# All tokens in grid order, and two groups' values projected with x as the stationary operand

## The chip, the cores and the metric

The kernel runs on one core of one Trainium2 chip. The metric is the device time of one execution in microseconds (us), the median of several runs. The profile is of one further execution, taken by the hardware profiler.

## The reference

Two layers of a bidirectional encoder over 1024 tokens of width 1024, in float32. The tokens form a grid of 16 rows of 64. Each layer projects the normed x into four head groups, attends in each, mixes the four outputs and runs a squared-ReLU MLP.

```python
for l in range(DEPTH):                       # 2
    h = rms_norm(x, norm1_g[l])
    proj = h @ w_in[l]                       # 1024 x 2400
    a_cq, a_ckv, a_kr, b_q, b_k, b_v, c_q, c_k, c_v, d_q, d_k, d_v = split(proj)
    y_a = mla_mixer(...)     # A: 4 heads, latent queries and keys, all 1024 keys
    y_b = diff_mixer(...)    # B: 4 heads, two softmaxes each, all 1024 keys
    y_c = swa_mixer(...)     # C: 4 heads, keys within 128 tokens of the query
    y_d = na_mixer(...)      # D: 4 heads, 8 rows x 16 columns of the 64-wide grid
    mix = concat([rms_norm(y_a), y_b, rms_norm(y_c), rms_norm(y_d)])
    x = x + mix @ w_out[l]
    x = x + square(relu(rms_norm(x, norm2_g[l]) @ w_up[l])) @ w_down[l]
return rms_norm(x, final_norm_g)
```

A, B and D don't care in which order the tokens stand, if the rotary tables, the masks and the result follow it. C is banded in natural order. D becomes banded with blocks of 128 when the tokens are put in grid order: eight columns of the grid (16 rows each) to a block.

## The kernel before

**Precision.** Every wide operand is kept as two float32r parts, high and low (`wh`, `wl` for weights, `xh`, `xl` for x, `both` for results on their way to DRAM). `passes` issues three matmuls for one product: high by high, high by low, low by high. ScalarE makes the high part (a copy), VectorE or GpSimd the low part (a subtraction).

**Projection.** x lies transposed in SBUF as eight pairs of tiles `xh`/`xl` of 128 features by 1024 tokens. `one(t, xs, ev)` projects 128 columns of `w_in`: two loads of 256 KB into `ws` (two buffers), split into `wh`/`wl`, and for each half of the tokens 24 matmuls with the weights stationary and 512 tokens moving, into one PSUM bank (`bank`, eight in all). The result is transposed, features by tokens. An eviction function takes it from there: `ev_rope` multiplies it with the rotary tables (`tabc`, `tabs`, which hold 1/rms of the tokens too) and adds; `ev_plain` multiplies with 1/rms (`rb`); `ev_grid` does the same for D and puts the tokens in grid order on the way. Queries and keys then go to DRAM (`qb`, `kb`, `qd`, ...) by `to_parts`. Values are needed with tokens on the partitions, so `to_values` transposes each half with four TensorE transposes against `ident` (`bank<-ident,part` in the profile), copies them out of PSUM on ScalarE and stores them (`vb`, `vd`, `vc`, `va`).

**Stages of a layer.** `open` computes the first wave: three weight tiles at once into six banks (`WAVES[0]`: B's queries, keys and values of heads 0 and 1), in two halves of the features, while the squares of x are summed; 1/rms (`rstd_cols`, `spread_here`) is known only when that is well under way, and the tables can be multiplied only then. `b1` is the second wave, `lat`, `pd`, `pc` the projections of A, D and C, `up` A's second stage; `b`, `d`, `c`, `a` are the attentions, `o1`, `o2` the output projection, then the MLP.

**Order.** All instructions are first recorded, with a due time for each stage (`SPAN`). A planner (`Plan.order`) then lists them engine by engine, by its own cost model and the due times, with a limited number of SBUF slots and PSUM banks. What it lists is fixed: on the chip each engine runs its list in order, and an instruction that waits holds all behind it. Every instruction is issued through one helper, so that all of them carry line 677 in the profile.

## Time and profile before

| | |
|---|---|
| time, median of 3 runs | 2522.41 us (2521.24 to 2526.48) |
| the profiled execution's own time | 2517.78 us |
| its span | 2516.0 us |
| TensorE (PE) busy | 2467.4 us, 98% |
| VectorE (DVE) busy | 1909.8 us, 76% |
| ScalarE (ACT) busy | 1290.5 us, 51% |
| GpSimd (POOL) busy | 379.7 us, 15% |
| DMA | 378.56 MB, 150 GB/s |

In the rows of the profile, PE is a matmul and PEld the load of its stationary operand; `bank<-xh,wh` is a matmul that reads the tiles xh and wh and writes a PSUM bank. In a timeline the columns are start, duration, engine, line, operation, names, shapes and, in brackets, how long the engine stood idle just before and what ended that. The first layer's attention and output projection take about 0 to 600 us, the second layer's 1250 to 1840 us; the MLPs lie between and behind.

### The profile page before, as it was taken

What the parts mean: (1) busy time and instruction counts of PE and PEld (TensorE: products, weight loads), DVE (VectorE), ACT (ScalarE), POOL (GpSimd) and SP (SyncE); (2) the same over time, 40 slices, a digit from 0 to 9 for tenths busy, and PEclk for the clock granted to TensorE, in tenths of its full rate; (3) what the DMA queues carried; (4) which work ended last, traced back from release to release, by engine and by line L of the source; (5) the groups of instructions that cost most, each with busy time, mean ns of one, the idle gap of its engine ahead of it and who ended that gap; (6) DMA issues with size and microseconds to landing.
All of it is one profiled execution on the core that took longest, in us unless ns stands there. A gap on an engine that the chain in (4) does not pass through costs nothing.

```text
span 2516.0 us, 35396 instructions
## 1 busy us (share of the span) xinstructions
PE 2467.4 (98%) x12332; PEld 1967.1 (78%) x12332; DVE 1909.8 (76%) x3576; ACT 1290.5 (51%) x2397; POOL 379.7 (15%) x258
## 2 busy tenths in 40 slices
PE   8999999999999999999999999999999999999998
PEld 6777776778888887888877777677788888888887
DVE  7767867775877779888777677677678777898887
ACT  4545757653644445444425456666455444444454
POOL 3323224213000000000042231332140000000000
PEclk9999999999999999999999999999999999999999
DMA  5534478622244457444154344885123444665431
GB/s 180 180 112 133 122 218 234 197 80 72 78 165 159 151 202 271 147 142 139 72 182 130 119 117 135 232 255 170 46 70 117 155 155 158 231 231 158 130 105 67
DMA packets 190514, 378.56 MB, mean 150 GB/s; under 512 B 24112, under 2 KB 36352, under 8 KB 190336
## 3 DMA queue, kind: packets, MB, share of 16 engines
q1 hardware_dynamic: 175360, 350.09, 44.6%
q10 hardware_dynamic: 14976, 26.22, 2.7%
q8 instruction: 97, 1.59, 0.3%
q14 instruction: 81, 0.66, 0.1%
HBM read 260.15 MB, written 116.07 MB: 150 GB/s over the span
## 4 chain that ended last, share of the span: by engine, by line
PE 83%; DVE 8%; DMA 4%; ACT 2%; issue 2%; SPq 1%; POOL 0%; DVEq 0%; POOLq 0%; ACTq 0%
PE bank L677 83%; DVE p L677 2%; DVE part L677 1%; SPq L677 1%; ACT p L677 1%; DVE x L677 1%; DMA a<-in_w_down 1%; DVE sq L677 1%; DMA acts<-ev 1%; DVE col L677 0%; DMA latp<-lat 0%; DMA c<-in_w_down 0%; DVE xl L677 0%; DVE ev L677 0%; DVE both L677 0%
## 5 line engine op out<-in xcount | busy, mean ns | idle before, releaser
L677 PE MATMUL bank<-far,wh 128*128 128x512 f32 (+1 forms) x2848 | 870.3, 387 | 1.1 <-ACT wh L677 0.6
L677 PEld LDWEIGHTS bank<-far,wh 128*128 128x128 f32 x2848 | 532.4, 188 | 110.5 <-ACT wh L677 1.4
L677 PE MATMUL bank<-far,wl 128*128 128x512 f32 (+1 forms) x1424 | 550.3, 387 | 2.7 <-DVE wl L677 2.7
L677 ACT ACTIVATE p<-p,col 128x1024 f32<-128x1024 f32 (+2 forms) x320 | 294.6, 921 | 196.3 <-DVE col L677 194.2
L677 POOL TENSOR_TENSOR wl<-ws,wh 128x512 fp32r<-128x512 f32 (+1 forms) x138 | 191.1, 1390 | 1180.2 <-ACT wh L677 1089.8
L677 PEld LDWEIGHTS bank<-far,wl 128*128 128x128 f32 x1424 | 267.4, 188 | 57.9 <-DVE wl L677 3.4
L677 PE MATMUL bank<-stack 96*128 96x512 f32 (+2 forms) x896 | 285.0, 395 | 5.0 <-DVE col L677 2.3
L677 DVE TENSOR_TENSOR x<-bank,x 128x512 f32<-128x512 f32 (+1 forms) x276 | 187.2, 680 | 121.9 <-PE bank L677 121.0
L677 PE MATMUL bank<-ident,p 128*128 128x128 f32 x1376 | 253.6, 276 | 10.4 <-DVE part L677 4.8
L677 PE MATMUL bank<-xh,wh 128*128 128x512 f32 x608 | 250.9, 413 | 3.1 <-ACT wh L677 2.6
L677 PE MATMUL bank<-xh,wl 128*128 128x512 f32 x608 | 250.6, 413 | 1.1 <-POOL wl L677 1.1
L677 PE MATMUL bank<-xl,wh 128*128 128x512 f32 x608 | 250.6, 412 | 0.0
L677 PEld LDWEIGHTS bank<-ident,p 128*128 128x128 f32 x1376 | 171.3, 141 | 59.5 <-issue 10.7
L677 PEld LDWEIGHTS bank<-stack 96*128 96x128 f32 (+1 forms) x896 | 159.3, 189 | 43.8 <-DVE col L677 12.1
L677 ACT ACTIVATE pt<-bank 128x512 f32<-128x512 f32 (+2 forms) x256 | 137.5, 556 | 82.9 <-PE bank L677 75.2
L677 DVE TENSOR_TENSOR wl<-raw,wh 128x512 fp32r<-128x512 f32 x224 | 150.3, 690 | 34.5 <-ACT wh L677 34.0
L677 PE MATMUL bank<-pt,v 128*64 128x256 f32 (+2 forms) x1344 | 173.1, 396 | 2.2 <-ACT pt L677 2.0
L677 ACT ACTIVATE ev<-ev 128x512 f32<-128x512 f32 x128 | 80.6, 632 | 160.3 <-DVE ev L677 155.8
L677 DVE CUSTOM_DVE_ANT_0 p<-bank,zero,col 128x512 f32<-128x512 f32 x192 | 143.8, 749 | 22.2 <-PE bank L677 5.1
L677 PE MATMUL bank<-mix,wh 128*128 128x512 f32 x512 | 160.3, 393 | 0.0
L677 DVE CUSTOM_DVE_ANT_0 p<-bank,zero 128x512 f32<-128x512 f32 x192 | 131.7, 686 | 35.4 <-PE bank L677 34.1
L677 ACT ACTIVATE wh<-raw 128x512 fp32r<-128x512 f32 x224 | 135.4, 621 | 23.8 <-ACT ev L677 10.5
(158 smaller groups left out, 3904.5 us busy)
## 6 DMA issues: line engine op xcount, KB each, us to landing
act<-acts SPq DMA_DIRECT2D x224, 256.0 KB
raw<-in_w_up SPq DMA_DIRECT2D x128, 256.0 KB
acts<-ev SPq DMA_DIRECT2D x128, 256.0 KB
acts<-ev ACTq DMA_DIRECT2D x96, 256.0 KB
ws<-in_w_in SPq DMA_DIRECT2D x76, 256.0 KB
c<-in_w_down SPq DMA_DIRECT2D x64, 256.0 KB
rz<-drows SPq DMA_DIRECT2D x40, 256.0 KB
ws<-in_w_out SPq DMA_DIRECT2D x40, 256.0 KB
```

Source lines behind the costliest of these rows:

```text
L677: getattr(s.eng.engine, s.op)(*[real(a) for a in s.args], **{k: real(a) for k, a in s.kw.items()})
```

## The change

x is put in grid order on the host, and the result is put back there. The rotary tables follow the same order. So D needs no reordering at its evictions (`ev_grid` goes, `ev_plain` takes its place), while C is put back in natural order at its own evictions: `ev_rope` and the new `ev_rows` collect two halves and write with a strided pattern (`by_rows`). The strided copies of the attention output and of the denominators (`rows_of`) move from D to C.

B's and D's values are no longer projected as four weight tiles (`T_BV`, `T_DV`). `values` loads their 512 columns as eight tiles `wv` of 128 features, all held at once, and for each of eight blocks of 128 tokens issues 24 matmuls with x stationary and the 512 weight columns moving. The result has tokens on the partitions already, so that no transpose follows; ScalarE takes it out of PSUM and multiplies with 1/rms, which is now one number per partition. The first wave gets B's second query tile in place of the values; `b1` has `values` and B's second key tile. `vb` and `vd` are stored as blocks of 128 tokens by 256 columns, and a head's values are loaded from there in pieces of 64 numbers (`head_of`).

```diff
-T_BQ, T_BK, T_BV = (3, 6), (4, 7), (5, 8)
-T_DQ, T_DK, T_DV = (9, 12), (10, 13), (11, 14)
+T_BQ, T_BK = (3, 5), (4, 6)
+T_DQ, T_DK = (7, 9), (8, 10)
...
+def grid_order():
+    return np.arange(S).reshape(16, 8, 8).transpose(1, 0, 2).ravel()
...
-    t = np.arange(S, dtype=np.float32)
+    t = grid_order().astype(np.float32)
...
-    out["x"] = i["x"][0].T.reshape(8, P, S)
+    out["x"] = i["x"][0].T[:, grid_order()].reshape(8, P, S)
+    out["w_v"] = np.concatenate([i["w_in"][:, :, c:c + 256] for c in (864, 2144)], 2).reshape(n, 8, P, 512)
...
-        qb, kb, vb = dr([2, 2, 4, 16, 2, S], "qb"), dr([2, 2, 4, 16, 2, S], "kb"), dr([4, P, 8, 64], "vb")
+        qb, kb, vb = dr([2, 2, 4, 16, 2, S], "qb"), dr([2, 2, 4, 16, 2, S], "kb"), dr([8, P, 256], "vb")
...
-                yield from one(T_DQ[t], xs, self.ev_grid(rb, self.to_parts(qd[:, t], 0.125)))
-                yield from one(T_DK[t], xs, self.ev_grid(rb, self.to_parts(kd[:, t])))
-                yield from one(T_DV[t], xs, self.ev_grid(rb, self.to_values(vd[2 * t:2 * t + 2])))
+                yield from one(T_DQ[t], xs, self.ev_plain(rb, self.to_parts(qd[:, t], 0.125)))
+                yield from one(T_DK[t], xs, self.ev_plain(rb, self.to_parts(kd[:, t])))
+
+        def values(r):
+            ws = []
+            for k in range(8):
+                st = self.wp.tile([P, 512], F, tag="ws", bufs=2, name="ws")
+                self.load(st, d["w_v"][l, k])
+                w = self.place.tile([P, 2, 512], R, tag="wv", bufs=8, name="wv")
+                self.split(w[:, 0], w[:, 1], st, eng=nc.gpsimd)
+                ws.append((w[:, 0], w[:, 1]))
+            for t in range(8):
+                ps, at = self.mm_ps(), slice(t * P, t * P + P)
+                for k, (x, w) in enumerate(zip(xs, ws)):
+                    self.passes(ps, (x[0][:, at], x[1][:, at]), w, slice(0, 512), k == 0, k == 7)
+                v = self.part()
+                nc.scalar.activation(v, ps, AF.Copy, scale=r[:, t:t + 1])
+                for dst, c in ((vb, 0), (vd, 256)):
+                    self.keep(dst[t], v[:, c:c + 256])
...
-                yield from one(T_CQ2[t], xs, self.ev_rope(tabs, qc[:, t]))
-            yield from one(T_CK, xs, self.ev_rope(tabs, kc))
-            yield from one(T_CV, xs, self.ev_plain(rb, self.to_values(vc)))
+                yield from one(T_CQ2[t], xs, self.ev_rope(tabs, qc[:, t], True))
+            yield from one(T_CK, xs, self.ev_rope(tabs, kc, True))
+            yield from one(T_CV, xs, self.ev_rows(rb, self.to_values(vc)))
...
-            for ev, b in zip(evacs_b(0), banks):
+            for dst, b in zip((qb[:, 0], kb[:, 0], qb[:, 1]), banks):
+                ev = self.ev_rope(tabs, dst)
...
-            for t, ev in zip(self.WAVES[1], evacs_b(1)):
-                run_all(one(t, xs, ev))
+            values(r)
+            run_all(one(T_BK[1], xs, self.ev_rope(tabs, kb[:, 1])))
...
-    WAVES = [(T_BQ[t], T_BK[t], T_BV[t]) for t in range(2)]
+    WAVES = [(T_BQ[0], T_BK[0], T_BQ[1])]
...
-        return self.place.tile([P, 512], F, tag="part", bufs=3, name="part")
+        return self.place.tile([P, 512], F, tag="part", bufs=4, name="part")
...
+    def by_rows(self, ys, n, *halves):
+        for i, y in enumerate(ys):
+            o = y.rearrange("p (r b c) -> p b r c", r=8, b=8)[:, n * 4:n * 4 + 4]
+            yield (o, *(t.rearrange("p (b r c) -> p b r c", b=4, r=16)[:, :, 8 * i:8 * i + 8] for t in halves))
...
+            for o, a, b in self.by_rows(ys, n, t1, t2):
+                self.tt(o, a, b, ALU.add, self.eng)
...
+    def head_of(self, v, h):
+        return v[:, :, h * 64:h * 64 + 64].rearrange("t p d -> p t d")
...
-            v = self.vtile(vb[2 * t + h2])
+            v = self.vtile(self.head_of(vb, 2 * t + h2))
...
-    return np.ascontiguousarray(y.reshape(DM, S).T)[None]
+    out = np.empty((1, S, DM), np.float32)
+    out[0, grid_order()] = y.reshape(DM, S).T
+    return out
```

Three places show what the planner makes of it. The first is TensorE in the first layer, around the end of the first wave. Before, a second weight tile follows the wave (`bank_107<-xh_275,wl` is of its second half of tokens), and the four transposes of B's values stand in its midst:

```order
L677 MATMUL bank_107<-xl_288,wh 128x512
L677 MATMUL bank_107<-xh_275,wl 128x512
L677 MATMUL bank_101<-ident,part 128x128 x4
L677 MATMUL bank_107<-xh_292,wh 128x512
L677 MATMUL bank_107<-xl_308,wh 128x512
```

After, the wave's last matmul (`bank_106<-xh_352,wl`) is followed by the first matmuls of `values`, each into another bank; banks 101 to 106 are those of the wave:

```order
L683 MATMUL bank_106<-xh_352,wl 128x512
L683 MATMUL bank_100<-wv,xh_239 128x512
L683 MATMUL bank_107<-wv,xh_239 128x512
L683 MATMUL bank_101<-wv,xh_239 128x512
L683 MATMUL bank_102<-wv,xh_239 128x512
L683 MATMUL bank_103<-wv,xh_239 128x512
L683 MATMUL bank_100<-wv,xh_239 128x512
L683 MATMUL bank_100<-wv,xl_245 128x512
L683 MATMUL bank_100<-wv,xh_262 128x512 x2
```

The transposes are gone, and in their place TensorE now asks for bank 103 five matmuls behind the wave's end, for bank 104 thirteen matmuls later, for bank 105 fifteen after that, and for bank 106 nineteen after that.

The second place is ScalarE and GpSimd at the same time. Before, ScalarE splits weights and rotated parts in turn, and GpSimd multiplies C's tables (`tabc`, `tabs`) behind seven weight splits:

```order
L677 ACTIVATE wh<-ws 128x512 x2
L677 ACTIVATE both<-part 128x512 x2
L677 ACTIVATE wh<-ws 128x512
L677 ACTIVATE both<-part 128x512 x2
L677 ACTIVATE part<-bank_101 128x512
...
L677 TENSOR_TENSOR wl<-ws,wh 128x512 x7
L677 TENSOR_TENSOR tabc<-tabc,rb 128x1024
L677 TENSOR_TENSOR tabs<-tabs,rb 128x1024
L677 TENSOR_TENSOR wl<-ws,wh 128x512 x4
L677 TENSOR_TENSOR part<-part 128x512
```

After, the splits of `wv` stand there, in ScalarE's list between those of the rotated parts:

```order
L683 ACTIVATE wv<-ws 128x512 x3
L683 ACTIVATE both<-part 128x512
L683 ACTIVATE wv<-ws 128x512 x2
L683 ACTIVATE both<-part 128x512 x2
L683 ACTIVATE wv<-ws 128x512 x2
...
L683 TENSOR_TENSOR wl<-ws,wh 128x512 x6
L683 TENSOR_TENSOR wv<-ws,wv 128x512 x8
L683 TENSOR_TENSOR wl<-ws,wh 128x512 x3
L683 TENSOR_TENSOR tabc<-tabc,rb 128x1024
L683 TENSOR_TENSOR tabs<-tabs,rb 128x1024
```

Eight splits of `wv` have moved ahead of C's tables on GpSimd, and five of the eight wait on ScalarE behind rotated parts.

The third place is TensorE in the second layer, again at the end of the first wave. Before, the second tile follows, with the transposes after five of its matmuls:

```order
L677 MATMUL bank_103<-xh_11109,wl 128x512
L677 MATMUL bank_100<-xh_11036,wh 128x512
L677 MATMUL bank_100<-xl_11071,wh 128x512
L677 MATMUL bank_100<-xh_11036,wl 128x512
L677 MATMUL bank_100<-xh_11058,wh 128x512
L677 MATMUL bank_100<-xl_11104,wh 128x512
L677 MATMUL bank_101<-ident,part 128x128 x4
```

After, seven banks get their first matmul of `values` in a row; banks 103, 106, 102, 104, 105 and 101 are those of the wave, in the order in which they are emptied:

```order
L683 MATMUL bank_101<-xh_11067,wl 128x512
L683 MATMUL bank_100<-wv,xh_10994 128x512
L683 MATMUL bank_107<-wv,xh_10994 128x512
L683 MATMUL bank_103<-wv,xh_10994 128x512
L683 MATMUL bank_106<-wv,xh_10994 128x512
L683 MATMUL bank_102<-wv,xh_10994 128x512
L683 MATMUL bank_104<-wv,xh_10994 128x512
L683 MATMUL bank_105<-wv,xh_10994 128x512
L683 MATMUL bank_100<-wv,xh_10994 128x512
```

The fifth bank of the wave (105) is asked for at the seventh matmul behind its end, and the sixth (101) eleven matmuls after that.

More of the change, by code (lines that the diff above doesn't have):

```diff
@@ L794, in rows_of @@
                 rows = slice(j * 8, j * 8 + 8)
-                flat = dr[rows].rearrange("a b -> (a b)").rearrange("(r b c) -> b r c", r=16, b=8)
-                self.store(flat, sb[rows].rearrange("b (r c) -> b r c", r=16))
+                flat = dr[rows].rearrange("a b -> (a b)").rearrange("(b i q c) -> i q b c", b=8, i=8, q=2)
+                for q in range(2):
+                    self.store(flat[:, q], sb[rows, q * 64:q * 64 + 64].rearrange("i (b c) -> i b c", b=8))
         else:
@@ L1085, in ev @@
             c, s = tabs
+            if rows and n == 0:
+                ys.extend([self.part(), self.part()])
             t1, t2 = self.part(), self.part()
@@ L1089, in ev @@
             self.tt(t2[64:128], ps[0:64], s[0:64, sl])
-            self.tt(t1, t1, t2, ALU.add, self.eng)
-            self.emit_parts(t1, [(dst[:, :, h, sl].rearrange("a p s -> p a s"), slice(h * 64, h * 64 + 64))
-                                 for h in range(2)])
+            if not rows:
+                self.tt(t1, t1, t2, ALU.add, self.eng)
+                out(n, t1)
+                return
+            for o, a, b in self.by_rows(ys, n, t1, t2):
+                self.tt(o, a, b, ALU.add, self.eng)
+            if n == 1:
+                for i, y in enumerate(ys):
+                    out(i, y)
         return ev
```

43 lines of the change are left out of this document (22 added, 21 removed).

## The prediction

> **What bounds the kernel now.** I read the page first, then TensorE's timeline and its waits around the places where the order changes, then the other engines there, then busy time by stage.
>
> ```profile
> PE 2467.4 (98%) x12332; PEld 1967.1 (78%) x12332; DVE 1909.8 (76%) x3576; ACT 1290.5 (51%) x2397; POOL 379.7 (15%) x258
> PE 83%; DVE 8%; DMA 4%; ACT 2%; issue 2%; SPq 1%; POOL 0%; DVEq 0%; POOLq 0%; ACTq 0%
> ```
>
> TensorE is busy for 98% of the span and carries 83% of the chain that ended last. So the change is worth what it takes from TensorE's list, plus or minus the time that TensorE stands idle. Busy time by stage (columns: the stage, its length, then busy time of PE, PEld, DVE, ACT and POOL with their counts, the granted clock, DMA share and GB/s) shows where it does:
>
> ```profile
> 0.00:600.00 600.00, 578.50 (x3220) 438.94 (x3221) 419.56 (x949) 340.03 (x664) 168.21 (x117) 0.99 0.52 155
> 600.00:1250.00 650.00, 648.12 (x2873) 536.40 (x2872) 525.65 (x817) 299.70 (x517) 21.26 (x14) 1.00 0.44 149
> 1250.00:1840.00 590.00, 575.86 (x3239) 439.36 (x3238) 416.15 (x934) 332.12 (x655) 168.27 (x112) 1.00 0.52 152
> ```
>
> The two attention stages, which the change reorders, leave TensorE idle for 21.5 and 14.1 us; the MLP between them for 1.9, and it keeps its instructions. All that moves lies in the first and third row.
>
> **The projections' own work.** Four weight tiles with two halves of 24 matmuls are 192 matmuls of 128x512 a layer; eight token blocks with 24 are 192 again, with stationary tiles of the same size. Nothing gained, nothing lost.
>
> **The transposes.** What goes is 32 transposes a layer, in groups of four. TensorE's timeline in the first layer:
>
> ```profile
> 39.60 0.48 PE L677 MATMUL bank<-xh,wh 128*128 128x512 f32 x1
> ...
> 55.12 0.39 PE L677 MATMUL bank<-xh,wl 128*128 128x512 f32 x1
> ...
> 57.16 0.39 PE L677 MATMUL bank<-xh,wl 128*128 128x512 f32 x1
> 60.22 0.66 PE L677 MATMUL bank<-ident,part 128*128 128x128 f32 x4 [2.68 <-DVE part L677]
> ...
> 61.88 0.60 PE L677 MATMUL bank<-ident,part 128*128 128x128 f32 x4
> ...
> 62.55 0.40 PE L677 MATMUL bank<-xh,wh 128*128 128x512 f32 x1
> ...
> 73.16 0.70 PE L677 MATMUL bank<-stack 96*128 96x512 f32 x2 [2.01 <-DMA stack<-kb]
> ```
>
> Durations overlap, so starts count: nine matmuls lie between 55.12 and 57.16, 0.227 us each. From 61.88 to 62.55 stand four transposes and one wide matmul: 0.67 - 0.23 = 0.44 us a group. Sixteen groups in two layers: 16 x 0.44 = **-7.0 us**. All of it lies on TensorE's own path; nothing hides it.
>
> **The waits ahead of them.** The transposes at 60.22 had waited 2.68 us for VectorE's eviction. The second layer has the same, after a wave of which 83 matmuls follow the broadcast of 1/rms and start at 1277.96:
>
> ```profile
> 1277.96 0.48 PE L677 MATMUL bank<-xl,wh 128*128 128x512 f32 x1
> ...
> 1300.19 0.66 PE L677 MATMUL bank<-ident,part 128*128 128x128 f32 x4 [2.01 <-DVE part L677]
> ```
>
> Both go: **-4.7 us**.
>
> **B's start.** At 73.16 above TensorE waits 2.01 us for B's first keys, with nothing else in its list. In the new order the first scores stand among the matmuls of `values`, 46 of them behind the last bank change, at about 77 us by the timetable below. SP issues all but one of the loads of those keys behind the store of the sixth bank's parts, so from about 69 us on, and they have some 3 us more than now: **-2.0 us**; if that cover is too thin, 0. Then come stages in which VectorE is nearly full:
>
> ```profile
> 54.00:60.00 6.00, 3.54 (x16) 2.61 (x14) 5.82 (x9) 1.03 (x2) 0.11 (x1) 1.00 0.57 153
> ...
> 84.00:90.00 6.00, 4.85 (x21) 3.35 (x22) 5.57 (x15) 3.15 (x7) 0.39 (x1) 1.00 0.94 296
> 90.00:96.00 6.00, 5.18 (x34) 3.24 (x33) 5.72 (x14) 4.27 (x8) 0.69 (x1) 1.00 0.02 6
> 1298.00:1304.00 6.00, 3.99 (x15) 3.03 (x15) 3.36 (x6) 1.75 (x3) 1.28 (x1) 0.74 0.81 234
> ```
>
> TensorE idles 1.15 + 0.82 = 2.0 us from 84 to 96, while VectorE also evicts two rotated tiles of `b1`. Afterwards it is one tile. I take half: **-1.0 us** (0 to -2).
>
> **The new waits: banks.** `values` starts when the wave ends, and its first matmuls ask for the banks that VectorE is still emptying. VectorE's and GpSimd's timelines there:
>
> ```profile
> 40.61 1.23 DVE L677 TENSOR_TENSOR tabc<-tabc,rb 128x1024 f32<-128x1024 f32 x1
> 41.75 3.43 DVE L677 TENSOR_TENSOR tabs<-tabs,rb 128x1024 f32<-128x1024 f32 x1
> 45.11 0.68 DVE L677 TENSOR_TENSOR part<-bank,tabc 128x512 f32<-128x512 f32 x1
> 45.80 1.39 DVE L677 TENSOR_TENSOR part<-bank,tabs 64x512 f32<-64x512 f32 x2
> ...
> 50.80 0.69 DVE L677 TENSOR_TENSOR part<-part 128x512 f32<-128x512 f32 x1
> ...
> 52.83 1.82 DVE L677 TENSOR_TENSOR both<-part,both 128x512 fp32r<-128x512 f32 x1
> ...
> 55.40 0.69 DVE L677 TENSOR_TENSOR part<-part 128x512 f32<-128x512 f32 x1
> ...
> 58.88 0.69 DVE L677 TENSOR_TENSOR part<-part 128x512 f32<-128x512 f32 x1
> ```
>
> ```profile
> 40.66 3.44 POOL L677 TENSOR_TENSOR tabc<-tabc,rb 128x1024 f32<-128x1024 f32 x1 [4.61 <-DVE rb L677]
> ...
> 52.81 1.30 POOL L677 TENSOR_TENSOR wl<-ws,wh 128x512 fp32r<-128x512 f32 x1 [3.65 <-issue]
> ```
>
> The same multiplication takes 1.23 us alone and 3.43 beside GpSimd's. In the new order GpSimd has splits of `wv` there, most of them earlier or later, so I start the evictions 2.0 us earlier: 43.1 instead of 45.1. A rotated bank takes 3.5 us (55.40 to 58.88), or 4.6 when one of GpSimd's splits falls on it (50.80 to 55.40, with the 1.82 us row inside). Five of the eight `wv` splits come during these evictions, one in a cycle; I take 4.2 us. The first bank is free 2.1 us after the start, at 45.2, and the others at 49.4, 53.6, 57.8, 62.0 and 66.2.
>
> TensorE ends the wave at 39.60 + 45 x 0.227 = 49.8. Its fifth matmul of `values` is ready at 50.7 and gets the third bank at 53.6 (2.9 us). Thirteen matmuls later, at 56.6, it asks for the fourth (1.2 us), fifteen later, at 61.2, for the fifth (0.8 us), nineteen later, at 66.3, for the sixth, which is free. Together 5 us; with 3.5 us a bank it is 2, with 4.6 it is 7, and 9 if the tables are still slowed. `wv` itself is not late by this: its last split follows the fifth rotated part and is wanted after the sixth bank.
>
> In the second layer the wave ends at 1277.96 + 83 x 0.227 = 1296.8. The broadcast rows there are the same, with evictions from 1281.3 if the tables are not slowed. At 4.2 us the fifth bank is free at 1300.2 and asked for at 1298.2 (2.0 us), the sixth at 1304.4 and asked for at 1302.7 (1.7 us). Together 3.7 us; 0 at 3.5 us a bank, 6 at 4.6, 8 with slow tables. Both layers: **+8.7 us** (2 to 17). All projections of the layer and B's scores are queued behind these waits on TensorE.
>
> [...] After the second layer's 2.01 us wait the granted clock is 0.74 for 6 us (1298:1304 above), 1.6 us lost; after 2.68 us in the first layer it stays at 1.00 (54:60). [...] The sum keeps 0, since that 1.6 us is in the time before as well.
>
> **The values' way back.** `vb` is now complete only after the eighth block, and each head loads it in 1,024 pieces of 64 numbers instead of 128 pieces of 512. Between the last matmul of `values` and the first product that needs a head's values stand 30 wide matmuls and 8 transposes in the first layer: 30 x 0.227 + 8 x 0.11 = 7.7 us of cover. No row shows such small pieces. A store and the load that depends on it are issued 3.0 us apart below, and B's keys, issued from 68.27 on, were waited for until 73.16:
>
> ```profile
> 68.27 2.87 SPq L677 DMA_DIRECT2D stack<-kb  x6
> ...
> 383.65 0.62 SPq L677 DMA_DIRECT2D lat<-both  x1
> ...
> 386.69 2.40 SPq L677 DMA_DIRECT2D latp<-lat  x4
> ```
>
> ```profile
> L677 ACT ACTIVATE part<-bank 128x512 f32<-128x512 f32 x28 | 16.2, 593 | 16.2 <-PE bank L677 16.2
> ```
>
> An eviction (0.6), two stores and their landing (3 to 4), the load (2 to 5) make 6 to 10 us: a wait of 0 to 2.5 in each layer, **+1.0 us** taken. [...]
>
> **Edits at nothing.** VectorE loses D's and B's value evictions:
>
> ```profile
> L677 DVE TENSOR_TENSOR part<-bank,rb 128x256 f32<-128x256 f32 x48 | 18.1, 419 | 24.6 <-PE bank L677 24.5
> ```
>
> Of these 48 eight remain, four wide ones are added, and a few rotations change engine: some 6 us less of work that TensorE's own list covers (0 to -2). C's strided additions on GpSimd (24 of 256 numbers instead of 12 of 512) stand on an engine that is 15% busy; they are hidden by the attention of B and D, and cost up to 2 us if VectorE waits for a free `part`. The strided copies that go from D to C keep their number.
>
> **The sum.** -7.0 - 4.7 - 2.0 - 1.0 + 8.7 + 1.0 = -5.0 us. On the profiled execution's 2517.8 that is 2512.8. The median of the runs is 4.6 us above it, and the same difference gives **2517.4 us**. A measurement here can tell about 0.2%, 5 us, from no change; the forecast lies at that edge.
>
> **The rivals.** *Banks come quickly* (22%): GpSimd's splits miss VectorE's additions, a bank takes 3.5 us, the new waits are 2 us instead of 8.7: 2511. For it: the earlier start; against it: the 1.82 us row shows that such meetings happen.
>
> *Banks come late in both layers* (22%, slower): 4.6 us a bank and slow tables, 17 us instead of 8.7, and 1.6 us of lower clock in each layer behind the longer waits, with 4 us for the values instead of 1: -5.0 + 8.3 + 3.2 + 3.0 = +9.5, 2532. It decides from 14 us of bank waits on, where the gain is used up. For it: ScalarE's list puts every split of `wv` right behind a rotated part, when VectorE does its two additions. Against it: in the first layer only one of the cycles seen is slow.
>
> *The saving is spent elsewhere* (18%): the freed 7 us of TensorE turn into waits for VectorE later in the attention, where the planner has dealt the order anew; the 35.6 us of idle time in the two stages is the room in which that happens, and then 2522 is left, within 3 us.
>
> The forecast keeps 38%: 26 of it beyond -5 us, 12 within. Faster: 26 + 22 + 2 = 50%. Same: 12 + 13 + 3 = 28%, of which 13 come from the saving spent and 3 from late banks of which only one layer has them. Slower: 19 + 3 = 22%. The range that leaves out one in ten at each end goes from 2505, quick banks and 6 us of reordering in its favour, to 2532.
>
> **What would show it.** Right: 64 fewer `bank<-ident,part`; no wait of `ident,part` at the wave's end; waits of `bank<-wv,xh` for VectorE's `part` of 2 to 3 us in each layer, 6 to 12 us together; scores of B starting with no wait for `stack<-kb`. Wrong: those waits near zero or above 14 us, TensorE's `pt,v` waiting for `v<-vb`, or more idle time in the stages from 100 to 500 us of each layer.

## The result, and the profile after

The changed kernel takes 2524.77 us (median of 20 runs, 2520.86 to 2529.50), the kernel before, run beside it, 2519.39 us (20 runs). The ratio is 1.0018, 95% interval 1.0012 to 1.0024: slower by 4.5 us by the ratio, where 5.0 us faster was forecast. The profiled execution took 2526.09 us (span 2524.3) against 2517.78 (2516.0) before. So the two traces lie 8.3 us apart, more than the kernels do: that of before is faster than its median, that of after slower than its own. A difference between the two traces is one pair of executions, and the runs of the changed kernel alone spread over 9 us.

The page's busy times, and the busy time of the same three stages:

```profile
PE 2474.2 (98%) x12268; PEld 1970.2 (78%) x12268; DVE 1897.7 (75%) x3548; ACT 1292.1 (51%) x2397; POOL 366.1 (15%) x262
```

```profile
0.00:600.00 600.00, 577.88 (x3182) 437.40 (x3183) 413.82 (x935) 340.21 (x663) 162.33 (x118) 0.99 0.52 155
600.00:1250.00 650.00, 647.76 (x2871) 536.12 (x2870) 524.05 (x815) 298.48 (x516) 22.00 (x15) 1.00 0.43 149
1250.00:1840.00 590.00, 575.51 (x3186) 437.65 (x3185) 407.31 (x917) 331.41 (x651) 157.82 (x113) 0.98 0.51 153
```

TensorE has 64 instructions fewer and is busy 6.8 us longer; VectorE is busy 12 us less. TensorE's timeline at the start of `values` in each layer, then VectorE's in the first:

```profile
49.56 1.07 PE L683 MATMUL bank<-wv,xh 128*128 128x512 f32 x4
52.96 0.73 PE L683 MATMUL bank<-wv,xh 128*128 128x512 f32 x2 [2.33 <-DVE part L683]
...
54.98 2.60 PE L683 MATMUL bank<-wv,xh 128*128 128x512 f32 x6
...
76.70 0.47 PE L683 MATMUL bank<-stack 96*128 96x512 f32 x1 [0.42 <-DMA stack<-kb]
...
101.85 0.50 PE L683 MATMUL bank<-stack 96*128 96x512 f32 x1 [2.03 <-DVE col L683]
...
1298.53 1.88 PE L683 MATMUL bank<-wv,xh 128*128 128x512 f32 x6
1304.42 1.22 PE L683 MATMUL bank<-wv,xh 128*128 128x512 f32 x2 [4.01 <-DVE part L683]
```

```profile
41.39 1.22 DVE L683 TENSOR_TENSOR tabs<-tabs,rb 128x1024 f32<-128x1024 f32 x1
42.53 0.68 DVE L683 TENSOR_TENSOR part<-bank,tabc 128x512 f32<-128x512 f32 x1
```

The bank waits are where the prediction put them: 2.33 and 4.01 us, both for VectorE's `part`. VectorE starts the evictions at 42.53 (43.1 was reckoned), B's keys are waited for 0.42 us instead of 2.01, and the waits ahead of the transposes at the wave's end are gone:

```profile
L683 PE MATMUL bank<-ident,part 128*128 128x128 f32 x48 | 8.3, 275 | 0.9 <-DVE part L683 0.9
```

No wait of `pt,v` for a load of `v` is in the list. What is new lies further back. Three places in each layer, read from the timeline as the start of the last matmul of a kind, cut the attention stage: the last projection, the last matmul of the latent parts (`latp`), the last of the output projection (`mix`). Lengths in us:

| kernel | to the last projection | to the last `latp` | to the last `mix` | second layer: the same three |
|---|---|---|---|---|
| before | 360.0 | 78.9 | 205.1 | 344.9, 76.5, 206.0 |
| after | 358.1 | 80.2 | 207.1 | 344.9, 79.1, 208.5 |

Up to the last projection the change gains 1.9 and 0 us; behind it, in the softmax of C and of the latent heads and in the output projection, it loses 3.3 and 5.1 us. The rest, some 2 us, is in the two MLPs. (The output projections end at 644 and 1886 us before the change, not at 600 and 1840 as the stages above have it, so the second of those rows does hold a piece of what the change reorders.)

The loss behind the second layer's last projection is not idle time. From the last projection to the last `mix` (columns as in the stages), before and after:

```profile
1604.00:1886.50 282.50, 276.53 (x1633) 210.73 (x1632) 199.61 (x428) 172.06 (x353) 92.25 (x61) 1.00 0.50 149
```

```profile
1605.60:1893.20 287.60, 282.09 (x1633) 214.83 (x1632) 199.26 (x428) 172.31 (x353) 91.88 (x61) 0.98 0.47 146
```

TensorE stands idle for 6.0 us before and 5.5 after; the same 1633 matmuls take 5.6 us longer, at a lower clock.

A second thing is new, the granted clock. Its mean over the runs is 0.9898, and 0.9933 in 107 runs of the kernel before, so that 25.7 us of clock are lost in a run (1 minus the clock, times the span) against 17.0. In the two traces it is 25.2 against 10.2: the trace of before, at 0.996, is at the upper end of those 107 runs (0.990 to 0.996), and so the two traces overstate the difference. Four stretches of the changed kernel, cut at the edges at which the clock changes (columns as in the stages above):

```profile
50.39:53.80 3.41, 1.08 (x6) 0.71 (x5) 3.28 (x6) 0.55 (x2) 0.00 (x0) 1.00 0.92 262
53.80:57.21 3.41, 3.41 (x10) 2.64 (x9) 3.33 (x4) 1.54 (x3) 2.31 (x2) 0.51 0.47 159
```

```profile
1637.57:1640.98 3.41, 2.96 (x21) 2.21 (x20) 1.62 (x4) 1.44 (x2) 0.27 (x1) 1.00 0.99 288
1640.98:1644.39 3.41, 2.83 (x14) 2.14 (x14) 3.22 (x9) 1.33 (x4) 2.02 (x2) 0.51 0.10 22
```

The first is the bank wait, and the stretch behind it is at half speed. The third is not idle at all: 2.96 of 3.41 us busy. But this is what runs there:

```profile
1638.79 0.73 PE L683 MATMUL bank<-latp,wh 128*128 128x512 f32 x2 [0.45 <-DMA latp<-lat]
1639.51 2.23 PE L683 MATMUL bank<-pairs,rz 128*128 128x2 f32 x16
```

Sixteen matmuls of two columns each: an occupied engine that streams almost nothing. The profiled execution has 13 half-speed stretches of 3.41 us between the first 5 us and its tail, the one before the change 4.

### The profile page after: what moved, and what is told of

Read it like the earlier page. It is cut to its first block, busy times and chain, and to the rows that moved or that the text cites. A ratio compares the mean times of both kernels' runs of the same rounds, so it can differ in the third digit from the quotient of the medians.

```text
span 2524.3 us, 35226 instructions
## 1 busy us (share of the span) xinstructions
PE 2474.2 (98%) x12268; PEld 1970.2 (78%) x12268; DVE 1897.7 (75%) x3548; ACT 1292.1 (51%) x2397; POOL 366.1 (15%) x262
## 2 busy tenths in 40 slices
DMA packets 205169, 378.55 MB, mean 150 GB/s; under 512 B 40816, under 2 KB 53056, under 8 KB 204992
## 3 DMA queue, kind: packets, MB, share of 16 engines
q1 hardware_dynamic: 190016, 350.09, 43.5%
## 4 chain that ended last, share of the span: by engine, by line
PE 85%; DVE 7%; DMA 3%; ACT 2%; issue 2%; SPq 0%; POOL 0%; DVEq 0%; ACTq 0%; POOLq 0%
PE bank L683 85%; DVE p L683 2%; DVE part L683 2%; ACT p L683 1%; DMA c<-in_w_down 1%; DVE x L683 1%; DMA acts<-ev 1%; DVE ev L683 0%; SPq L683 0%; DVE both L683 0%; DMA a<-in_w_down 0%; DMA latp<-lat 0%; DVE col L683 0%; ACT mix L683 0%; DMA ws<-in_w_in 0%
## 5 line engine op out<-in xcount | busy, mean ns | idle before, releaser
L683 POOL TENSOR_TENSOR wl<-ws,wh 128x512 fp32r<-128x512 f32 (+1 forms) x122 | 168.0, 1382 | 1100.8 <-ACT wh L683 1027.1
L683 PE MATMUL bank<-xh,wh 128*128 128x512 f32 x480 | 200.2, 417 | 4.0 <-ACT wh L683 2.5
L683 PE MATMUL bank<-xh,wl 128*128 128x512 f32 x480 | 198.1, 414 | 1.2 <-POOL wl L683 1.2
L683 PE MATMUL bank<-xl,wh 128*128 128x512 f32 x480 | 198.2, 413 | 0.0
L683 PEld LDWEIGHTS bank<-stack 96*128 96x128 f32 (+1 forms) x896 | 159.8, 190 | 47.8 <-DVE col L683 12.8
```

The source lines that it names most:

```text
L683: getattr(s.eng.engine, s.op)(*[real(a) for a in s.args], **{k: real(a) for k, a in s.kw.items()})
```

## The experiments

Ratios are to the kernel before on the same chip, and 0.001 is 2.5 us. "Clock lost" is the mean over the runs. Four kernels (e8, e10, e11, e15) leave out C's reordering, so that C attends to other tokens with the same matmuls; they show what that work costs and are no solutions. Theory at the start: the transposes' gain is real, and the slow stretches, from the new bank waits and from an attention dealt anew, take it back. Rivals: the bank waits alone; the attention's order alone; the grid order.

**e1, blocks one after the other.**

```
-    FIRM = {"wh", "wl", "wah", "wal", "wkeep", "stack", "v"}
+    FIRM = {"wh", "wl", "wah", "wal", "wkeep", "stack", "v", "wv"}
```

> The changed kernel, with one word more: wv joins the planner's list of weights that need no lead of 2 us (FIRM), so that the matmuls of values run block after block (24 on a bank, then the next) instead of one on every bank in turn. Theory (clock): the changed kernel has 13 half-speed stretches of 3.41 us before its last block against 4 before the change, 1.7 us lost in each; three of them (at 53.8 and from 1303.1 us) come from the bank waits at the start of values. Here the third bank is asked for some 5 us later in each layer, the waits of bank<-wv,xh for part go from 6.3 us to under 2, and the three slow stretches with them: 2524.8 - 4.5 - 5.1 = 2515, range 2512 to 2519. Rival 1 (waits alone, the clock costs nothing): -4.5 us, 2520. Rival 2 (the loss comes from the attention stages alone, dealt anew): within 3 us of 2524.8, with the waits gone all the same.

Measured: 1.0076 (1.0062 to 1.0089), clock lost 29.4 us. The waits for banks went as expected, and other waits came; its list of waits:

```profile
PE bank L683 <- DVE p L683: 5.5, 4, 2.2
PE bank L683 <- ACT wv L683: 5.1, 4, 1.7
...
PE bank L683 <- DVE part L683: 3.7, 6, 0.9
```

The first block now wants all eight tiles of `wv` at once, and B's first transposes then wait for VectorE (2.17 us in each layer). Taking away the waits at the start of `values` gains nothing by itself: the first theory's first half fails.

**e2, the grid order alone** (projections, tiles and transposes of the values as before the change; the rest as after).

```
-            values(r)
-            run_all(one(T_BK[1], xs, self.ev_rope(tabs, kb[:, 1])))
+            for t, ev in zip(self.WAVES[1], evacs_b(1)):
+                run_all(one(t, xs, ev))
```

> Only the one half of the change: all tokens in grid order and C's tiles put in natural order at eviction, while B's and D's values are projected with the weights stationary and turned by 64 transposes as before (four buffers for part stay). Theory (clock, most of it from the way the values are made and from what is dealt anew behind it): the transposes (7.0) and the waits ahead of them at the wave's end (4.7) are back, the bank waits (6.3) and most of the additional slow stretches are gone: near the kernel before, 2516 to 2523. Rival (the grid order and C's additions at eviction carry the loss): 2525 to 2533, with waits of TensorE in the stretch 200 to 400 us.

Measured: 1.0061 (1.0049 to 1.0074), 15 us slower than before. The rival holds: this half carries the loss, and the values' half takes 11 us of it back.

**e3 and e4, the same instructions dealt anew.**

```
-    LATE = 700
+    LATE = 720
```

> The changed kernel with one number of the planner altered: it reckons a dependent transfer 720 ns late instead of 700. Every instruction is the same, the order is dealt anew. Theory (a 3.41 us stretch in which the streamed columns fill less than about a third is followed by one at half speed, and which stretches these are depends on how the attention falls): the number of slow stretches moves by up to 4 either way, the time by up to 7 us, with the loss at the start of values kept. Rival (the loss is in the structure): within 1.5 us of 2524.8.

> The kernel before the change with the same one number altered, 720 ns instead of 700: same instructions, another order. Theory (deals differ): the time moves by 2 to 6 us from 2519.4, more likely up than down, since the deal of before is a good one with 4 slow stretches; the number of slow stretches accounts for most of the difference at 1.7 us each. Rival (structure decides): within 1.5 us of 2519.4.

Measured: 1.0022 (1.0014 to 1.0031) and 1.0003 (0.9994 to 1.0012). So slight a push of the planner moves neither. It was very slight: by the traces, TensorE's list has another matmul, by tiles and shape, in 105 of 12,268 places (e3) and in 22 of 12,332 (e4), where a fourth buffer (e9 below) changes 866. So these two runs do not show that an order dealt anew on that scale is free.

**e5, e6, e7, zeros in the gaps.** The instructions keep their order; `emit` adds matmuls of zeros at listed places.

```
+                    for _ in range(FILL.get(count, 0)):
+                        v = list(groups.values())[-1]   # a bank being summed
+                        w = self.zero.real()
+                        s.eng.engine.matmul(v.real(), w, w[:, 0:1].broadcast_to([P, 512]), start=False, stop=False)
```

> The changed kernel in exactly its own order, with matmuls of zeros (128x512, added to a bank that is being summed anyway) in the two bank waits at the start of values: 6 behind the fourth matmul of values in the first layer, 18 in the second. No wait ends sooner; only TensorE streams columns in it. Clock theory (a stretch of 3.41 us with less than about 0.3 of its time filled by columns is followed by one at half speed): the slow stretches at 53.8 and 1303.1 to 1309.9 us go, mean granted clock up by 0.001 to 0.002, time 1.5 to 5 us lower: 2520 to 2523. Rival (the waits alone cost, the clock there is hidden by VectorE's lateness): within 1 us of 2524.8.

> The changed kernel in its own order with 70 such matmuls of zeros in 24 places, at the waits and between the runs of very small matmuls where the trace has less than 0.36 of a 3.41 us stretch filled and a bank is being summed (not in the softmax sums at 359 and 1606 us, where none is). They delay the rest by 0.4 us by the trace's gaps. Clock theory: the clock lost falls from 25.7 us (mean of the runs, 1 minus the granted clock times the span) to about 10; the time falls by 7 (if half of the lost clock shows in the time, as the spread of runs of one kernel has it) to 15 us: 2510 to 2518. Rival (the clock only mirrors waits and costs little by itself): 2524 to 2526.

> The kernel before the change, the same treatment by its own trace: 43 matmuls of zeros in 19 places. Clock theory: its lost clock falls from 15.6 to about 9 us and its time by 3 to 6 us: 2514 to 2517. If the clock is all that turned the forecast of -5 into +5, the changed kernel with zeros is 4 to 6 us faster than this one; if the change has lost time elsewhere as well (the grid order), it is within 2 us of it or slower. Rival (clock costs little): 2519 to 2521.

Measured: e5 1.0007 (0.9997 to 1.0017), clock lost 18.3 us; e6 1.0010 (1.0001 to 1.0018), 10.5 us; e7 1.0006 (0.9997 to 1.0015), 11.7 us. The clock follows the zeros as the theory says; the time hardly does. TensorE's timeline of e5 shows why:

```profile
51.70 1.47 PE L690 MATMUL bank<-zero 128*128 128x512 f32 x6
54.20 0.73 PE L698 MATMUL bank<-wv,xh 128*128 128x512 f32 x2 [1.03 <-DVE part L698]
...
58.75 0.73 PE L698 MATMUL bank<-wv,xh 128*128 128x512 f32 x2 [1.31 <-DVE part L698]
...
1298.05 4.09 PE L690 MATMUL bank<-zero 128*128 128x512 f32 x18
1302.23 0.73 PE L698 MATMUL bank<-wv,xh 128*128 128x512 f32 x2
...
1306.75 0.50 PE L698 MATMUL bank<-wv,xh 128*128 128x512 f32 x1 [1.73 <-DVE part L698]
```

At full speed TensorE comes to the next bank sooner and waits there, 1.31 and 1.73 us: VectorE's evictions set the pace, and the slow stretch had only filled a wait. In e6 70 zeros of 0.219 us (the time between the starts of two of them in the traces) are 15.3 us of work. Its busy times:

```profile
PE 2480.6 (98%) x12338; PEld 1975.7 (78%) x12338; DVE 1897.0 (75%) x3548; ACT 1292.4 (51%) x2397; POOL 367.2 (15%) x262
```

TensorE's busy time grew by 6.4 (2480.6 from 2474.2) and its idle time fell by 8.0 (42.1 from 50.1). So the other matmuls took 8.9 us less at the better clock, and 7.3 us of zeros came to lie on the path: what the clock gives, the zeros take. The spread of the runs gives a second estimate: in 278 runs of these kernels, each against its kernel's mean, 1 us more of lost clock goes with 0.46 us more time. Of the 8.7 us of clock that the changed kernel loses more, some 4 us would show in the time. With zeros the two kernels lose about the same (10.5 and 11.7 us), and the changed one is still 1 us slower by the ratios, within some 3, with 27 zeros more to carry. So the clock accounts for a part of the miss; e2 says which half of the change brings it.

**e8, C not reordered.**

```
-                yield from one(T_CQ2[t], xs, self.ev_rope(tabs, qc[:, t], True))
+                yield from one(T_CQ2[t], xs, self.ev_rope(tabs, qc[:, t]))
...
-            self.denominators(z, rz, 2)
+            self.denominators(z, rz)
```

> The changed kernel without the reordering of C: C's projections are evicted in the order of the tokens as they come (ev_rope and ev_plain as for B), its products and its denominators are written without the turn into grid order. C's windows then lie over tokens in grid order, so this part of the result is another; the matmuls are the same. If C's reordering carries the loss of the half that is in grid order (it took 15 us alone): 5 to 12 us faster than the changed kernel, 2513 to 2520. If not (the loss is in how the attention is dealt in either case): within 3 us of 2524.8.

Measured: 1.0004 (0.9995 to 1.0013), 3.5 us faster than the changed kernel: between the two expectations.

**e9, e10, e11: the fourth buffer and C's reordering, apart.** e9 is the kernel before with one number changed; e10 is e2 with e8's edit, e11 the same with three buffers.

```
-        return self.place.tile([P, 512], F, tag="part", bufs=3, name="part")
+        return self.place.tile([P, 512], F, tag="part", bufs=4, name="part")
```

> The kernel before the change with four buffers for part in place of three, which the change needs for C's eviction; nothing else. If the fourth buffer carries the loss of the half in grid order (it lets the evictions run further ahead and takes one of the 19 tiles of half size from the softmax), the time is up by 5 to 15 us, 2525 to 2535. If not, within 2 us of 2520.

> The half in grid order alone (e2), without the reordering of C (its tokens stay in grid order, so this part of the result is another). Against the kernel before, D's strided evictions are gone, and there are four buffers for part. If C's reordering carries the 15 us of e2: 2518 to 2523. If the loss lies in how the planner deals the attention, or in the fourth buffer: 2530 to 2536.

> The same with three buffers for part: all that is left against the kernel before is that D is not turned into grid order at its eviction and its output. Less work for VectorE and ScalarE by 2 to 4 us and nothing more for anyone: 2517 to 2521 if the fourth buffer or C's reordering carried the loss; if it is over 2525 with less work and the same buffers, the loss is in the deal alone.

Measured: e9 1.0055 (1.0043 to 1.0068); e10 1.0019 (1.0010 to 1.0028); e11 1.0003 (0.9994 to 1.0012). The grid order itself, with D no longer turned, costs and gains nothing that can be told (e11). A fourth buffer alone costs the kernel before 14 us. The stretches of 80 and 206 us behind the last projection, busy times of the kernel before and then of e9:

```profile
360.00:440.00 80.00, 73.67 (x455) 51.76 (x455) 56.42 (x146) 55.37 (x148) 38.16 (x25) 0.98 0.82 246
440.00:646.00 206.00, 205.54 (x1191) 161.31 (x1188) 146.98 (x286) 118.61 (x209) 54.26 (x37) 1.00 0.37 109
```

```profile
360.00:440.00 80.00, 72.94 (x431) 51.91 (x432) 54.67 (x144) 51.83 (x140) 36.84 (x24) 0.94 0.73 225
440.00:646.00 206.00, 204.00 (x1184) 158.51 (x1181) 143.73 (x281) 116.88 (x208) 54.36 (x37) 1.00 0.39 114
```

In the same 80 us TensorE gets 431 matmuls done instead of 455. It is hardly less busy (72.94 us in place of 73.67); the granted clock is 0.94 instead of 0.98. It is the place where the changed kernel loses too.

**e12, the key tile first.**

```
-            values(r)
             run_all(one(T_BK[1], xs, self.ev_rope(tabs, kb[:, 1])))
+            values(r)
```

> The changed kernel with the two steps of b1 exchanged: B's second key tile (48 matmuls in the two banks that are free at the wave's end, 10.9 us) ahead of values, so that VectorE has emptied three more banks when values asks for them. Theory (the bank waits at the start of values are VectorE's rotations, and cost their 6 us): the waits of bank<-wv,xh go from 6.3 us to under 2, with two to three slow stretches of the clock; 2518 to 2522. Rival (TensorE meets VectorE a few us later, since the rotations of a fourth pair of banks stand in VectorE's list before it reaches B's scores): within 2 us of 2524.8, with waits of bank<-wv or of B's first transposes for VectorE.

Measured: 1.0051 (1.0037 to 1.0065). Neither: the waits of `wv` for `part` are still there (0.60 and 2.29 us in the first layer), and B's softmax comes late; from its list of waits:

```profile
PE bank L683 <- DVE p L683: 7.3, 3, 3.2
```

**e13 to e16: three buffers.** C's rows get a ring of two tiles of half size (`tag="yrow", bufs=2`), `part` goes back to three; e13 is the changed kernel so, e14 is e2 so; e15 is e8 with three buffers, without that ring; e16 is e12 with e13's edit.

> The changed kernel with three buffers for part again; the two tiles in which C's rows are put together, for which the fourth was needed, get a ring of their own (two of half size). Every instruction stays. Theory (the fourth buffer lets evictions run ahead, so that projections end sooner and leave the softmax of C and of the latent heads less to be hidden by; in the ten kernels with four buffers the stretch from the last projection to the last matmul of the latent parts takes 80.6 and 80.9 us in the two layers and the one behind it to the end of the output projection 207.9 in each, in the four with three buffers 79.7, 77.1 and 205.8): 6 us less than the changed kernel, 2516 to 2520. Rival (any new deal costs or gains at random, and the buffer is one way to throw the dice): anywhere from 2521 to 2532.

> The half in grid order alone (e2: values still by 64 transposes) with three buffers for part and C's two rows in a ring of their own. Theory of the buffer: most of e2's 15 us are gone, 2519 to 2524. Rival (grid order or C's reordering carries them, the buffer only in the kernel before): 2529 to 2536.

> The changed kernel with three buffers for part and without C's reordering (that part of the result is another). Against e11 (2520.9), which has the same buffers and the same C, only the values differ. The forecast's sum for that is -5.0 us, and the slow stretches of the clock at the start of values give back 0 to 3: 2515 to 2519. Rival (the 64 transposes lay beside VectorE's work as the waits do, and their end gains nothing): 2520 to 2523.

> e13 with the two steps of b1 exchanged as in e12. If the bank waits at the start of values cost by themselves: 2 to 5 us below e13. If, as in e12, B's first softmax then waits for VectorE instead: 2 to 8 us above it.

Measured: e13 1.0015 (1.0007 to 1.0024), e14 1.0042 (1.0030 to 1.0054), e15 **0.9978 (0.9968 to 0.9987)**, e16 1.0076 (1.0064 to 1.0088). The buffer alone is not the cause: with three, C's reordering still costs 9 to 10 us (e13 against e15, e14 against e11), a price that includes the two tiles of half size which e13 and e14 hold for it. e16 is 15 us slower than e13, beyond both of its expectations: its waits at the start of `values` are 5.0 us in place of 6.3, and TensorE's waits for `p`, 0.8 us in e13, come to 6.9. So it does not tell what the bank waits are worth. The values' half is worth 6 us in the same surroundings (e15 against e11), and that with its bank waits as they are; e15's second layer:

```profile
1298.38 1.22 PE L683 MATMUL bank<-wv,xh 128*128 128x512 f32 x2 [4.01 <-DVE part L683]
```

**e17, e18: are tiles of half size short?** e17 is the kernel before with one of them less; e18 is the changed kernel with three buffers and C's rows as halves of a full tile.

```
-    PLACES = {"pair": 40, "half": 19, "row": 3, "col": 30, "bank": 8}
+    PLACES = {"pair": 40, "half": 18, "row": 3, "col": 30, "bank": 8}
```

> The kernel before with 18 tiles of half size (128x512) to deal out in place of 19. If the fourth buffer and C's held rows cost because they keep such tiles from the softmax (p, its transposes, the evicted scores), this costs about what the fourth buffer did: 2526 to 2536, with the loss between the last projection and the output projection. If the tiles are not short, the time stays within 3 us of 2521, and the loss of the others is a matter of order alone.

> The changed kernel with three buffers for part, C's two rows held as the halves of one tile of full size (128x1024, a ring of one). All work of the change is in it. If tiles of half size are what C's rows take from the softmax: near e15, which has no reordering: 2515 to 2519, faster than both kernels. If C's reordering costs by itself (each tile is finished only after its second half, and its queries and keys come later to the attention that they feed): 2522 to 2530.

Measured: e17 1.0043 (1.0030 to 1.0057), e18 1.0040 (1.0025 to 1.0055). One tile less costs 11 us, so the kernel before has none to spare; but freeing them does not help the changed kernel. e18 is slower than either expectation had it, and 6 us slower than e13. Short tiles of half size would explain what the fourth buffer costs; for C's rows they do not suffice. Whether the full tile of e18 was itself wanted elsewhere, no run shows.

The four pairs that differ in one thing each, from the ratios, in us (each within 3 to 4):

| surroundings | values' half | | surroundings | C's reordering |
|---|---|---|---|---|
| C plain, three buffers (e11, e15) | -6.3 | | old values, three (e11, e14) | +9.8 |
| C plain, four (e10, e8) | -3.8 | | old values, four (e10, e2) | +10.6 |
| C reordered, three (e14, e13) | -6.8 | | new values, three (e15, e13) | +9.3 |
| C reordered, four (e2, after) | -10.8 | | new values, four (e8, after) | +3.5 |

And the stages of some of them, as in the first table:

| kernel | first layer | second layer |
|---|---|---|
| e11 | 360.6, 80.3, 205.6 | 345.8, 76.6, 205.6 |
| e15 | 355.9, 78.2, 205.8 | 343.1, 81.1, 205.7 |
| e13 | 354.8, 81.5, 207.1 | 350.0, 79.8, 207.1 |
| e9 | 358.2, 82.8, 207.2 | 345.3, 84.9, 208.9 |
| e17 | 358.7, 83.2, 207.3 | 344.3, 79.9, 209.4 |
| e18 | 356.5, 81.7, 208.6 | 349.3, 81.7, 208.5 |

## Why the prediction was wrong

The sum was for the wrong half. Its six terms, from the transposes to the values' way back, are all of the values' half, and together they say -5.0 us; that half alone, against its nearest like, measured -6.3 (-3.8 to -10.8 over four surroundings).

The traces allow a second account. In the 17 of them without added zeros, TensorE's busy time is a constant, plus 0.85 us for each us of clock lost in that execution, plus 0.11 us for each `bank<-ident,part`; this fit, an estimate, meets each trace within 1.7 us. From the trace before to the trace after:

| | forecast | traces |
|---|---|---|
| transposes | -7.0 | -7.2 (64 fewer, by the fit) |
| TensorE's idle time (all waits and B's start) | +2.0 (-4.7 - 2.0 - 1.0 + 8.7 + 1.0) | +1.5 (48.6 to 50.1) |
| lost clock | 0 | +12.8 (15.0 us more lost, by the fit) |
| not explained | | +1.2 |
| span | -5.0 | +8.3 |

Work and waits came out nearly as forecast in their sums, though not one by one; what the sum lacked shows as a lower clock. By the means of the runs (8.7 us more lost) the last term is some 7 us of busy time rather than 12.8, and of that some 4 us show in the time, because waits get shorter when TensorE is slower: at full speed e5 has waits of 1.31 and 1.73 us where the changed kernel, in or just behind a slow stretch, has none. The fit says how the loss appears, not what brings it about; for that stand the experiments. Term by term:

- *Transposes, -7.0, and waits ahead of them, -4.7*: the instructions and waits are gone as forecast (x48 left). No run timed them by themselves; the fit gives -7.2 for the first.
- *B's start*: 0.42 us of wait left instead of none. The relief of VectorE came whole, and was given back 6 us later in a wait of 2.03 us for `col` (101.85). TensorE from 84 to 96 us:

```profile
84.00:90.00 6.00, 6.00 (x28) 4.88 (x27) 4.11 (x12) 3.01 (x5) 0.33 (x1) 1.00 0.48 148
90.00:96.00 6.00, 6.00 (x30) 4.91 (x29) 4.82 (x13) 3.23 (x6) 2.07 (x1) 1.00 0.25 74
```

- *Bank waits, +8.7*: 6.3 us as listed, 2.33 and 4.01 where 5 and 3.7 stood, for the reason given. In the second layer all of it falls on the fifth bank, for which 2.0 was reckoned. In the first layer the half-speed stretch behind hides the later ones (e5 shows one, 1.31 us).
- *Values' way back, +1.0*: nothing. The trace has 40,816 pieces under 512 B, 16,704 more than before, and TensorE has no wait for them (the prediction has it that no row shows such small pieces; the page before counts 24,112):

```profile
DMA packets 205169, 378.55 MB, mean 150 GB/s; under 512 B 40816, under 2 KB 53056, under 8 KB 204992
```

So the loads are covered here. The 4 us that the rival of late banks takes for the values (3.0 us in its sum) are shown by no run; in the trace after, no wait stands in their place.

- *The lower clock behind the waits, 0*: **mis-sized.** The sum kept 0 because the second layer's 1.6 us were in the time before as well; but the clock lost 8.7 us more in the mean, and of the 13 slow stretches in the trace only three stand behind the bank waits. Behind the bank waits themselves, raising it gained 2.8 us by the ratios (e5, whose interval overlaps the changed kernel's), since VectorE set the pace there.
- *Edits at nothing*: **the step that failed.** C's additions were costed by their engine's time ("an engine that is 15% busy"), and the fourth buffer stands in no term at all. The engine's time is borne out; GpSimd's groups before and after, of which 12 and 24 are C's:

```profile
L677 POOL TENSOR_TENSOR part<-part 128x512 f32<-128x512 f32 x24 | 30.8, 1284 | 77.5 <-DVE part L677 77.5
```

```profile
L683 POOL TENSOR_TENSOR part<-part 128x256 f32<-128x256 f32 x24 | 18.2, 779 | 46.3 <-DVE part L683 46.3
```

That is 18.2 us in place of 12 x 1.284 = 15.4, on an engine with time to spare. But e2 is 15 us slower than before, and e11 leaves of that only C's reordering and the buffer: 3.5 to 10.6 us for the one, 14 for the other in the kernel before (0.8 to 6.5 in the four pairs in grid order). Both change the order that the planner deals for everything behind: TensorE's list differs in 866 places between e9 and the kernel before, and in 1166 between e14 and e11. That they do so by when evictions end and which tiles are free, and that this order is what costs, is argued and not shown. What they cost appears in two forms: in the traces e9 loses 21 us more clock than the kernel before (9 in the mean of the runs) with as much idle time (49.2 and 48.6 us), while e14 loses no more clock than e11 and has 14 us more idle time (57.5 and 43.5). In the changed kernel a small part lies far behind C's evictions, in waits of a microsecond, 1.9 us in place of 0.4; TensorE's waits between 440 us and the end of the output projection, before and then after (the third, of 0.19 us, left out):

```profile
465.69 0.83 PE L677 MATMUL bank<-ones,sq 128*128 128x1 f32 x6 [0.37 <-DVE sq L677]
```

```profile
501.48 1.05 PE L683 MATMUL bank<-ones,sq 128*128 128x1 f32 x8 [0.66 <-DVE sq L683]
530.44 0.44 PE L683 MATMUL bank<-ident,p 128*128 128x128 f32 x2 [1.05 <-ACT pt L683]
```

Of the rivals, the third, *the saving is spent elsewhere*, comes nearest, but only in place: it looked behind the projections, at an order dealt anew. Its mechanism, freed time that turns into waits for VectorE, did not happen: the values' half kept its gain in all four surroundings, TensorE's waits for VectorE went from 26.4 to 28.4 us in all, and its idle time from 100 to 500 us of each layer, which the prediction named as a sign, stayed (20.3 and 20.5 us, both layers together). That its 2522, within 3 us, takes in 2524.77 is luck: the kernel before, measured again beside it, was itself 3 us lower, and against that the change costs 4.5.

Not settled is by which step C's reordering acts. That its rows are held until a tile's second half is evicted, and so reach C's attention later, fits e18; no run took that alone away. Nor is it settled how much is accident, since a new order can cost by itself: e1, e12 and e16, which order `values` otherwise, are 8 to 15 us slower than the kernels that they start from, with new waits of TensorE. Against mere accident speaks that e11, whose list differs from the kernel before's in 640 places, costs nothing, and that C's reordering costs, and the values' half gains, in all four surroundings. No run of the whole computation beat the kernel before; e15, without C's reordering, shows that there are 5.5 us to be had if C can be fed otherwise.

## What to carry to other kernels

Where a planner or pools set the order, an edit that costs no engine any time, a ring of four instead of three or a tile held over two evictions, can cost more than the edit that the change is about; so give each such edit a run of its own before adding it to a sum, and in the surroundings where it will stand: the fourth buffer cost 14 us in the old kernel and 1 to 6 in the kernels in grid order. Split a change with two halves: here one loses 15 us alone, the other takes 11 of them back, and the total shows neither. Count TensorE's idle time and its lost clock apart; an engine that was about as busy as before was slower in e9 (72.94 us busy in place of 73.67, 431 matmuls done in place of 455, at a clock of 0.94 in place of 0.98). And read a low clock together with who sets the pace in that stretch: behind the bank waits, where VectorE set it, raising the clock gained 2.8 us by the ratios, with intervals that overlap (e5).

## What the hardware showed

In these traces the granted clock goes by columns streamed rather than by idleness. In the 20 traces at hand I cut the time at the clock's own 3.41 us edges, left out the first 5 and the last 20 us, and added up the columns of the matmuls that start in each stretch at full speed, at 512 columns in 0.219 us (the time between the starts of two matmuls of zeros).

| share of the stretch filled by columns | next stretch at half speed |
|---|---|
| under 0.24 | 59 of 59 |
| 0.24 to 0.30 | 48 of 66 |
| 0.30 to 0.36 | 33 of 62 |
| 0.36 to 0.42 | 21 of 90 |
| 0.42 to 0.5 | 6 of 209 |
| over 0.5 | none of 13,920 |

With the edges moved by 0.1 us the counts shift by up to nine between neighbouring rows below 0.5; the last stays at none. TensorE's busy share divides them less well: of the stretches in which it was busy for 80% or more, 44 of 14,022 were followed by half speed. So a wait of 2.33 us within one stretch was followed by half speed (50.39 to 53.80 above, 1.08 of 3.41 us busy), and so was a run of sixteen two-column matmuls with hardly a wait (1637.57 to 1640.98, 2.96 of 3.41 us busy). In the trace after, every spell at one speed, up to the tail, is a whole number of 3.41 us (the longest 264), and every one is at full speed or at half (granted clock 1.0 or 0.5).
